# An FFN on one core: the down projection as seven block products, chained partial sums, and norm operands from unscaled sums

## The chip, the cores and the metric

The kernel runs on one core of a Trainium2 chip. The metric is device time in microseconds for one execution; before the change it is 2420.82 us, the median of three runs (2419.04 to 2423.86).

## The reference

Two layers of an encoder are applied to 256 + 512 = 768 token rows (two sequences, same weights), width 1024, in float32:

```python
h = rms_norm(x, g_mix[l]); proj = h @ w_in[l]
# attention on q, k, v of proj; a gated convolution branch on u; gates from gl
x = x + (ga * a + gc * c) @ w_out[l]
h2 = rms_norm(x, g_ffn[l])
gate, up = jnp.split(h2 @ w_gu[l], 2, axis=-1)
x = x + (jax.nn.silu(gate) * up) @ w_down[l]
```

and a last `rms_norm`. The change is in the last three lines: the FFN has 2816 inner columns, worked on as 22 chunks of 128.

## The kernel before

Everything is kept transposed: feature rows on the 128 partitions, the 768 tokens along the free dimension, in two halves of 384 (`HALVES`). A float32 product is made as three matmul passes (`PASSES`) over operands that are split into a rounded part `hi` and a remainder `lo`: hi x hi, hi x lo, lo x hi. The rounding is a ScalarE copy (`act`, line 211), the remainder a subtraction (`sub_lo`, line 214) on POOL for weights and on VectorE or POOL for activations. Operations of VectorE go through a helper and show as line 133.

Weights arrive as 512 KB `Stage` tiles by DMA on SP's queue. A `Unit` is one such tile split into `hi` and `lo` of 1024 columns. A `Quarter` is 512 columns of `hi` and 512 of `lo`, made from one block of a `Quad` (two stages seen as 2 x 2 blocks) or from a sum of blocks; `Quad.total` makes these sums on VectorE. `Weights.pump` loads stages and splits units ahead of use, as long as at most `N_WH` = 8 buffers are live, one split at a time, `W_STEP` of the program's own clock apart. The order of instructions on each queue is the order in which the Python program emits them; `Clock.at` and `Clock.later` place work some microseconds of that clock later, and `tick`, after each `yield` of a body, emits what is due and then calls `pump`.

The gate/up product of a chunk is done as a 2 x 2 x 2 block product with seven block products instead of eight (`seven`, `gu_body`): 7 x 4 x 3 = 84 matmuls of 384 columns. Product 2 is added in the bank of product 1 and product 3 in that of product 5; other sums are made on VectorE when the products come out of PSUM. Chunks 0 and 1 are done together at the start, interleaved; the others one by one. `finish` multiplies silu(gate) by up and splits the result into `acthi` and `actlo`.

The down projection (`down_body`) takes two chunks at a time: 8 output tiles x 2 token ranges (256 and 512 columns) x 2 chunks x 3 passes = 96 matmuls, each result added into the residual `xs` by VectorE. It follows the next gate/up chunk. The last block of a layer takes four chunks (18 to 21), and each `xs` tile that it completes goes into the next norm.

`ffn_norm` makes the operands of the seven products: first half (products 1 and 2) when the first half's scale is known, second half afterwards: operands 4, sums 5, then differences 6, 7 and 3. `Norm.finish` makes the scale: a matmul for the variance, a power on POOL, a transpose on TensorE (`n2var`, `n2R` in the rows), then the scalings on VectorE.

## Time and profile before

| | |
|---|---|
| median of three runs | 2420.82 us |
| the profiled execution | 2421.99 us, span 2420.2 us |
| mean granted TensorE clock | 0.973 |
| TensorE matmul busy | 2274.7 us (94%) |
| VectorE busy | 1669.6 us (69%) |
| POOL busy | 1203.7 us (50%) |
| ScalarE busy | 1008.5 us (42%) |

The span runs from the first to the last instruction. PE is TensorE, PEld its weight loads, DVE VectorE, ACT ScalarE, POOL GpSimd. The FFN lies at about 677 to 1210 us (layer 0) and 1875 to 2409 us (layer 1). Matmuls are pipelined, so that the busy time of one (0.34 us for 384 columns) overlaps that of the next.

### The profile page before, as it was taken

What the parts mean: (1) busy time and instruction counts of PE and PEld (TensorE: products, weight loads), DVE (VectorE), ACT (ScalarE), POOL (GpSimd) and SP (SyncE); (2) the same over time, 40 slices, a digit from 0 to 9 for tenths busy, and PEclk for the clock granted to TensorE, in tenths of its full rate; (3) what the DMA queues carried; (4) which work ended last, traced back from release to release, by engine and by line L of the source; (5) the groups of instructions that cost most, each with busy time, mean ns of one, the idle gap of its engine ahead of it and who ended that gap; (6) DMA issues with size and microseconds to landing.
All of it is one profiled execution on the core that took longest, in us unless ns stands there. A gap on an engine that the chain in (4) does not pass through costs nothing.

```text
span 2420.2 us, 34516 instructions
## 1 busy us (share of the span) xinstructions
PE 2274.7 (94%) x13516; PEld 2101.4 (87%) x13516; DVE 1669.6 (69%) x2272; ACT 1008.5 (42%) x1985; POOL 1203.7 (50%) x864
## 2 busy tenths in 40 slices
...
DMA packets 58019, 177.14 MB, mean 73 GB/s; under 512 B 6528, under 2 KB 13696, under 8 KB 57856
## 3 DMA queue, kind: packets, MB, share of 16 engines
...
q14 instruction: 57, 0.47, 0.1%
...
## 4 chain that ended last, share of the span: by engine, by line
PE 57%; DVE 31%; ACT 4%; POOL 4%; issue 3%; DMA 1%; POOLq 0%; SPq 0%; DVEq 0%; ACTq 0%
DVE L_y L133 22%; PE L_d L203 15%; PE L_c L203 5%; PE L_o L203 4%; PE L_gl L203 4%; PE L_f150m L473 1%; PE L_f70m L473 1%; PE L_f90m L473 1%; PE L_f130m L473 1%; PE L_f50m L473 1%; PE L_f190m L473 1%; PE L_f110m L473 1%; PE L_f170m L473 1%; PE L_f200m L473 1%; PE L_f210m L473 1%
## 5 line engine op out<-in xcount | busy, mean ns | idle before, releaser
L133 DVE SCALAR_TENSOR_TENSOR L_y<-L_z,vec,L_y 128x783 f32<-128x783 f32 x480 | 624.0, 1334 | 2.5
L214 POOL TENSOR_TENSOR wq_L_wgu_0m<-T_L_wgu,wq_L_wgu_0m 128x512 fp32r<-128x512 f32 x168 | 235.4, 1421 | 395.0 <-ACT wq_L_wgu_0m L211 222.2
L211 ACT ACTIVATE wq_L_wgu_0m<-T_L_wgu 128x512 fp32r<-128x512 f32 x168 | 99.7, 625 | 484.8 <-DVE T_L_wgu L133 478.2
L203 PE MATMUL L_d<-L_acthi,lo_L_wd 128*128 128x256 f32 (+1 forms) x704 | 237.8, 338 | 4.5 <-POOL lo_L_wd L214 4.5
L133 DVE TENSOR_TENSOR L_x<-L_d,L_x 128x256 f32<-128x256 f32 (+1 forms) x344 | 183.7, 556 | 82.3 <-PE L_d L203 80.5
L203 PE MATMUL L_d<-L_acthi,hi_L_wd 128*128 128x256 f32 (+1 forms) x704 | 237.1, 337 | 0.0
L203 PE MATMUL L_d<-L_actlo,hi_L_wd 128*128 128x256 f32 (+1 forms) x704 | 236.9, 337 | 0.0
L214 POOL TENSOR_TENSOR wq_L_wgu_0m<-st_L_wgu,wq_L_wgu_0m 128x512 fp32r<-128x512 f32 x126 | 167.3, 1346 | 43.4 <-ACT wq_L_wgu_0m L211 39.6
L203 PE MATMUL L_gl<-L_h1h,hi_L_wgl 128*128 128x512 f32 (+1 forms) x512 | 178.6, 349 | 0.6 <-DVE L_h1t4m L133 0.6
L214 POOL TENSOR_TENSOR lo_L_wgl<-st_L_wgl,hi_L_wgl 128x1024 fp32r<-128x1024 f32 x32 | 104.6, 3276 | 147.8 <-ACT hi_L_wgl L211 147.8
L203 PE MATMUL L_gl<-L_h1h,lo_L_wgl 128*128 128x512 f32 (+1 forms) x512 | 174.9, 342 | 0.0
L203 PE MATMUL L_gl<-L_h1l,hi_L_wgl 128*128 128x512 f32 (+1 forms) x512 | 174.6, 341 | 0.0
L203 PEld LDWEIGHTS L_d<-L_acthi,lo_L_wd 128*128 128x128 f32 x704 | 132.3, 188 | 20.3 <-POOL lo_L_wd L214 5.1
L203 PEld LDWEIGHTS L_d<-L_actlo,hi_L_wd 128*128 128x128 f32 x704 | 132.3, 188 | 14.8
L203 PEld LDWEIGHTS L_d<-L_acthi,hi_L_wd 128*128 128x128 f32 x704 | 132.4, 188 | 14.4
L214 POOL TENSOR_TENSOR lo_L_wqkv<-st_L_wqkv,hi_L_wqkv 128x1024 fp32r<-128x1024 f32 x24 | 67.4, 2815 | 125.7 <-ACT hi_L_wqkv L211 109.3
L133 DVE TENSOR_TENSOR L_silu<-L_silu,L_fu 128x384 f32<-128x384 f32 x88 | 88.7, 1010 | 44.7 <-ACT L_silu L211 43.2
L214 POOL TENSOR_TENSOR lo_L_wd<-st_L_wd,hi_L_wd 128x1024 fp32r<-128x1024 f32 x44 | 105.0, 2405 | 11.6 <-ACT hi_L_wd L211 9.0
L203 PEld LDWEIGHTS L_gl<-L_h1h,lo_L_wgl 128*128 128x128 f32 x512 | 98.1, 192 | 11.4
L203 PEld LDWEIGHTS L_gl<-L_h1h,hi_L_wgl 128*128 128x128 f32 x512 | 98.3, 192 | 10.4 <-DVE L_h1t4m L133 0.8
L203 PEld LDWEIGHTS L_gl<-L_h1l,hi_L_wgl 128*128 128x128 f32 x512 | 98.5, 192 | 9.7
L214 POOL TENSOR_TENSOR lo_L_wu<-st_L_wu,hi_L_wu 128x1024 fp32r<-128x1024 f32 (+1 forms) x32 | 82.9, 2594 | 47.3 <-ACT hi_L_wu L211 47.3
...
## 6 DMA issues: line engine op xcount, KB each, us to landing
st_L_wgu<-w_gu SPq DMA_DIRECT2D x88, 512.0 KB, 4.2
st_L_wd<-w_down SPq DMA_DIRECT2D x44, 512.0 KB, 4.1
st_L_wu<-w_a SPq DMA_DIRECT2D x32, 512.0 KB, 3.5
st_L_wgl<-w_a SPq DMA_DIRECT2D x32, 512.0 KB, 3.4
st_L_wqkv<-w_qkv SPq DMA_DIRECT2D x24, 512.0 KB, 3.5
st_L_wpw<-w_pw SPq DMA_DIRECT2D x16, 512.0 KB, 3.6
st_L_wo<-w_out SPq DMA_DIRECT2D x16, 512.0 KB, 3.7
...
```

Of the source, the lines that this page charges most:

```text
L133: return f(out, *args, **kw)
L203: nc.tensor.matmul(out, lhsT, rhs, start=start, stop=stop)
L211: nc.scalar.activation(out, in_, func, **kw)
L214: engine.tensor_tensor(lo, x, hi.bitcast(F32), op=ALU.subtract)
L473: nc.tensor.matmul(ps, w[a][:, k * P:(k + 1) * P], h.cols(m, k, b), start=at == m and k == 0 and p == 0, stop=k == KH - 1 and p == 2, skip ...
```

## The change

- Chunks 0 to 19 of the down projection are taken four at a time (`down7`): the contraction (4 chunks) is two halves of two chunks, the output 4 + 4 tiles, the tokens 384 + 384, and the 2 x 2 x 2 block product is made with seven products, in the order 1, 7, 6, 4, 5, 2, 3. Each product has 4 banks, and each bank takes 2 x 3 matmuls of 384 columns.
- Products 6, 5 and 3 are added in product 1's banks and product 4 in product 7's (`CHAIN`); the partial sum is added to the residual after each product. Gate/up uses the same chain, with ScalarE copying the first partial sums out; the pair of chunks 0 and 1 has its own (`CHAIN_TWO`).
- The weights of these down blocks are quarters, with sums. The activations of chunks 0 to 19 are kept unsplit; the operands of the seven products are sums and differences of them (`total`), split into `hi` and `lo` in `prepare`.
- Stages, units and quarters share one pool of 12 buffers; two more stages may be loaded ahead; quarters follow each other after 0.9 instead of 1.45 of the program's clock.
- In the FFN norm the sums of the second half are made from the unscaled residual (`before`) while the output projection runs, and are multiplied by the scale afterwards; products are asked for in the order 1, 2, 5, 6, 7, 3, 4.
- The last block of a layer takes two chunks (20 and 21) in the old way.

```diff
--- before.py
+++ after.py
-                self.tile = wpool.tile([P, 1024], F32, name="st_" + self.name, tag="ws", bufs=N_WS)
+                self.tile = wpool.tile([P, 1024], F32, name="st_" + self.name, tag="w", bufs=N_W)
...
-                if self.loaded < len(self.stages) and self.staged < N_WS:
+                ahead = self.live <= N_WH - 2 and self.ready < len(self.all) and self.all[self.ready].size == 1
+                if self.loaded < len(self.stages) and self.staged < N_WS + 2 * ahead:
...
-                assert self.live + w.size <= N_WH
+                assert self.live + w.size + max(self.staged, N_WS) <= N_W
                 self.live += w.size
...
-                self.staged -= w.last
+                self.staged -= sum(stage.last is w for stage in w.stages)
...
-                self.next = max(self.next, clock.now + W_STEP * w.step / 2)
+                self.next = max(self.next, clock.now + W_STEP[w.size - 1])
...
-        def seven(ws, order, h, ready, name, done):
+        def seven(ws, order, chain, h, ready, name, done):
...
-                at = {2: 1, 3: 5}.get(m, m)
+                at = chain.get(m, m)
...
+                if p in self.own:
+                    self.own[p][0](j)
...
-                for j, f in enumerate([scale(j) for j in range(KC + 1)] + self.more[p]):
-                    steps.append(((N_STEPS[3][0] + each[0] * j, N_STEPS[3][1] + each[1] * j), f))
+                after = lambda j: each[0] * j if p not in self.own else N_OWN[0] * j + N_OWN[1] * max(0, j - KH)
+                if p in self.own:
+                    scales = [lambda f=f: f(rstd[0][:, :n]) for f in self.own[p][1]]
+                    more = [lambda f=f: f(rstd[0][:, :n]) for f in self.more[p]]
+                else:
+                    scales, more = [scale(j) for j in range(KC + 1)], self.more[p]
+                for j, f in enumerate(scales + more):
+                    steps.append(((N_STEPS[3][0] + after(j), N_STEPS[3][1] + each[1] * j), f))
...
+                def before(j):
+
+                    k = j % KH
+                    if j < KH:
+                        if k % 2 == 0:
+                            tot[k] = tot[k + 1] = Z(nm(f"hs{k}"))
+                        act(part(k), y.xs[j][:, second], AF.Copy, scale=gain(j))
+                    else:
+                        vector.scalar_tensor_tensor(part(k), y.xs[j][:, second], gain(j), part(k),
+                                                    op0=ALU.mult, op1=ALU.add)
+
+                def low(m, k, t, engine):
+                    norm.low()
+                    norm.lows.append(cut(m, k, t, engine))
+
+                def total(k):
+                    def f(r):
+                        vector.tensor_tensor(part(k), part(k), r, op=ALU.mult)
+                        low(5, k, part(k), vector if k % 2 else nc.gpsimd)
+                    return f
+
                 def more(m, k):
-                    def f():
-                        a11, a12, a21, s = to(k, 0), to(k + KH, 0), to(k, 1), part(k)
-                        d, x, z = {6: (s, s, a11), 7: (a21, a11, a21), 3: (a12, a12, s)}[m]
-                        vector.tensor_tensor(d, x, z, op=ALU.subtract)
-                        norm.low()
-                        norm.lows.append(cut(m, k, d, vector if k % 2 else nc.gpsimd))
+                    def f(r):
+                        a11, a12, s = to(k, 0), to(k + KH, 0), part(k)
+                        if m == 4:
+                            t = to(k + KH, 1)
+                            vector.scalar_tensor_tensor(t, y.xs[k + KH][:, second], gain(k + KH), r,
+                                                        op0=ALU.mult, op1=ALU.mult)
+                        elif m == 7:
+                            t = to(k, 1)
+                            vector.scalar_tensor_tensor(t, y.xs[k][:, second], gain(k), r, op0=ALU.mult, op1=ALU.mult)
+                            vector.tensor_tensor(t, a11, t, op=ALU.subtract)
+                        else:
+                            t, x, z = {6: (s, s, a11), 3: (a12, a12, s)}[m]
+                            vector.tensor_tensor(t, x, z, op=ALU.subtract)
+                        low(m, k, t, vector if k % 2 else nc.gpsimd)
                     return f
 
-                norm = Norm(nm("n2"), y.xs, lambda j: vcol(l, V_GFFN, j), HALVES, out, to=to,
-                            order=[range(KC), [*range(KH, KC), *range(KH)]],
-                            more=[[], [more(m, k) for m in (6, 7, 3) for k in range(KH)]], each=((0.7, 0.0), (0.55, 0.0)))
+                norm = Norm(nm("n2"), y.xs, gain, HALVES, out, to=to,
+                            more=[[], [more(m, k) for m in (6, 7, 3, 4) for k in range(KH)]], each=((0.7, 0.0), (0.55, 0.0)),
+                            own={1: (before, [total(k) for k in range(KH)])})
                 return norm
 
...
+                def done_one(m, e, ps):
                     c = cs[e]
-                    bank = lambda i: banks[e, i][:, :HN]
-                    first, second = slice(0, HN), slice(HN, T)
                     if m == 1:
-                        z = Z(nm(f"fz{c}"))
-                        tmp[e] = z[:, :HN], z[:, HN:T]
-                        act(tmp[e][0], bank(1))
+                        y.silu[c] = U(nm(f"silu{c}"))
+                        act(y.silu[c][:, first], ps)
+                        return
+                    g = y.silu[c]
+                    if m == 7:
+                        y.up[c] = Z(nm(f"fu{c}"))[:, :HN]
+                        act(y.up[c], ps)
+                    elif m == 6:
+                        act(g[:, second], ps)
+                    elif m == 4:
+                        add(g[:, second], ps)
+                        clock.at(0.8, lambda: silu(c, second))
+                    elif m == 5:
+                        add(y.up[c], ps)
+                        clock.at(0.2, lambda: times(c, second, y.up.pop(c)))
                     elif m == 2:
-                        if c not in y.silu:
-                            y.silu[c] = U(nm(f"silu{c}"))
-                        act(y.silu[c][:, first], bank(1), AF.Silu)
+                        add(g[:, first], ps)
+                        clock.at(0.8, lambda: silu(c, first))
+                    else:
+                        times(c, first, ps)
+                        finish(c)
+
...
+                def finish(c):
+                    g = y.acts[c] = y.silu.pop(c)
+                    if c in y.after:
+                        y.after.pop(c)()
+                    if c >= PLAIN:
+                        hi, lo = y.acts[c] = U(nm(f"acthi{c}"), F32R), U(nm(f"actlo{c}"), F32R)
+
+                        def parts():
+                            act(hi, g)
+                            clock.at(1.0, lambda: sub_lo(vector, lo, g, hi))
+                        clock.at(1.5, parts)
 
...
+            def down_cut(stages, r, c):
+                return stages[r - 1].tile[:, (c - 1) * 512:c * 512]
+
+            def down7(order, c0):
+
+
+                pairs = ((c0, c0 + 1), (c0 + 2, c0 + 3))
+                ops, banks, jobs, src = {}, {}, {}, {}
+                half = lambda t, i: t[:, i * HN:(i + 1) * HN]
+                ms = [m for m, e in order if e == 0]
+
+                def operand(m, e):
+
+                    a, b = (y.acts.get(c) for c in pairs[e])
+                    if m in (1, 2, 4):
+                        return {1: lambda: half(a, 0), 2: lambda: half(b, 0), 4: lambda: half(b, 1)}[m]()
+                    s = half(y.dsum, e)
+                    d, x, z, op = {7: lambda: (s, half(a, 0), half(a, 1), ALU.subtract),
+                                   6: lambda: (s, half(b, 1), s, ALU.subtract),
+                                   5: lambda: (half(a, 0), half(a, 0), s, ALU.add),
+                                   3: lambda: (s, half(b, 0), s, ALU.subtract)}[m]()
+                    vector.tensor_tensor(d, x, z, op=op)
+                    return d
+
+                def total(m):
+                    if m == 7:
+                        y.dsum = U(nm(f"dS{c0}"))
+                    src[m] = [operand(m, e) for e in range(2)]
+
+                def prepare(m):
+                    ops[m] = U(nm(f"dh{c0}_{m}"), F32R), U(nm(f"dl{c0}_{m}"), F32R)
+                    jobs[m] = []
+                    for e, x in enumerate(src[m]):
+                        hi, lo = (half(t, e) for t in ops[m])
+                        act(hi, x)
+                        jobs[m].append(clock.later(0.5 + 0.4 * e, lambda x=x, hi=hi, lo=lo: sub_lo(vector, lo, x, hi)))
+
+                def first():
+                    total(1)
+                    total(7)
+                    prepare(1)
+                    clock.at(1.0, lambda: prepare(7))
+
+                def done(m, j, bank):
+                    x = {1: (j, 0), 2: (j, 0), 7: (j + KH, 1), 5: (j + KH, 1), 6: (j, 1), 4: (j, 1), 3: (j + KH, 0)}[m]
+                    x = half(y.xs[x[0]], x[1])
+                    vector.tensor_tensor(x, bank, x, op=ALU.add)
+
+                def body(ws):
+                    for n, m in enumerate(ms):
+                        w = [ws[2 * n], ws[2 * n + 1]]
+                        for f in jobs[m]:
+                            f()
+                        at = CHAIN.get(m, m)
+                        for j in range(KH):
+                            if at == m:
+                                banks[m, j] = PS(nm(f"d{c0}m{m}_{j}"))
+                            ps = banks[at, j][:, :HN]
+                            for e in range(2):
+                                for p, (a, b) in enumerate(PASSES):
+                                    nc.tensor.matmul(ps, w[e][a][:, j * P:(j + 1) * P], half(ops[m][b], e),
+                                                     start=at == m and e == 0 and p == 0, stop=e == 1 and p == 2,
+                                                     skip_group_check=at != m)
+                                    clock.now += HN / 2400.0
+                            if j == KH - 1:
+                                ws.free(2 * n, 2 * n + 1)
+                            done(m, j, ps)
+                            if j == 0 and 0 < n < len(ms) - 1:
+                                prepare(ms[n + 1])
+                            if j == 1 and n < len(ms) - 2:
+                                total(ms[n + 2])
+                            yield
+                    for c in range(c0, c0 + 4):
+                        y.acts.pop(c)
+                tail = c0 == PLAIN - 4
+                y.after[PLAIN if tail else c0 + 2] = lambda: clock.at(
+                    D_AHEAD[tail], first)
                 return body
 
             def down_body(*cs):
...
                         order = [(es, j, p) for p in range(len(parts))
-                                 for es in ((chunks,) if p and l == L - 1 else (chunks[:2], chunks[2:])) for j in range(KC)]
...
             def add_gu(*cs):
-                order = [(m, e) for m in (1, 4, 5, 6, 7, 2, 3) for e in range(1)]
-                if len(cs) > 1:
-                    order = [(m, e) for m in (1, 2, 4, 5, 6, 7, 3) for e in range(len(cs))]
+                ms, chain = (ORDER, CHAIN) if len(cs) == 1 else (ORDER_TWO, CHAIN_TWO)
+                order = [(m, e) for m in ms for e in range(len(cs))]
                 units = weights.add_quads(nm(f"wgu{cs[0]}"), [[w_gu[l, b + c] for b in (0, NFF)] for c in cs],
                                           gu_cut, order)
-                stream.put([(l, f"gu:{c}") for c in cs], units, gu_body(order, *cs))
+                stream.put([(l, f"gu:{c}") for c in cs], units, gu_body(order, chain, *cs))
+
+            def add_down7(c0):
+                order = [(m, e) for m in ORDER for e in range(2)]
+                units = weights.add_quads(nm(f"wd{c0}"), [[w_down[l, c0 + 2 * e + i] for i in range(2)] for e in range(2)],
+                                          down_cut, order)
+                stream.put([(l, f"down:{c0}")], units, down7(order, c0))
 
             def add_down(*cs):
                 stream.add([(l, f"down:{c}") for c in cs], nm(f"wd{cs[0]}"), [w_down[l, c + e] for c in cs for e in range(2)],
                            down_body(*cs))
 
             add_gu(0, 1)
-            for c in range(2, NFF, 2):
+            for c in range(2, NFF):
                 add_gu(c)
-                if c < NFF - 2:
-                    add_down(c - 2)
-                add_gu(c + 1)
-            add_down(NFF - 4, NFF - 2)
+                if c % 4 == 3 and c < PLAIN - 1:
+                    add_down7(c - 3)
+            add_down7(PLAIN - 4)
+            add_down(PLAIN)
             return y
 
         def sigmoids(y):
...
+D_AHEAD = (4.0, 8.0)
+
+ORDER, CHAIN = (1, 7, 6, 4, 5, 2, 3), {6: 1, 5: 1, 3: 1, 4: 7}
+ORDER_TWO, CHAIN_TWO = (1, 2, 5, 6, 7, 3, 4), {6: 1, 7: 1, 4: 1, 3: 5}
...
+PLAIN = 20
...
-W_STEP = 2.9
+W_STEP = (0.9, 2.9)
...
+N_OWN = (0.5, 0.45)
...
+N_W = 12
```

## Rows read from the trace of the kernel before

**Rows 1.** The page, part 1: busy time and its share of the span

```profile
PE 2274.7 (94%) x13516; PEld 2101.4 (87%) x13516; DVE 1669.6 (69%) x2272; ACT 1008.5 (42%) x1985; POOL 1203.7 (50%) x864
```

**Rows 2.** The chain of waits, FFN of layer 0: start us, us, what

```profile
838.72 16.74 PE L_d L203 x96
870.23 14.62 PE L_f80m L473 x84
```

**Rows 3.** Busy time by stage, FFN of layer 0 (stage, length, engines, clock, DMA)

```profile
839.00:1162.00 323.00, 323.00 (x1848) 306.82 (x1847) 179.05 (x283) 96.97 (x169) 166.29 (x114) 1.00 0.20 66
```

**Rows 4.** Waits of TensorE, 650 to 730 us: total, times, longest

```profile
PE L_f00m L473 <- POOL L_h L214: 3.0, 3, 2.0
...
PE L_f00m L473 <- ACT wq_L_wgu_0m L211: 2.0, 1, 2.0
PE L_f01m L473 <- ACT wq_L_wgu_1m L211: 1.2, 1, 1.2
PE L_f01m L473 <- POOL wq_L_wgu_1m L214: 1.1, 2, 0.8
...
PE L_f00m L473 <- POOL wq_L_wgu_0m L214: 0.8, 1, 0.8
```

**Rows 5.** Busy time by stage, the FFN's start after the second scale

```profile
688.00:729.00 41.00, 32.94 (x141) 29.39 (x141) 35.08 (x48) 18.35 (x35) 29.48 (x23) 0.81 0.11 39
```

**Rows 6.** Timeline of TensorE at the seam: start, us, line, what, idle before

```profile
1221.99 0.66 PE L207 MATMUL L_n1R<-ident,L_n1rb 128*128 128x128 f32 x4 [2.60 <-DVE L_n1rb L133]
```

**Rows 7.** Timeline of TensorE at the end of the kernel

```profile
2410.24 0.89 PE L203 MATMUL nfvar<-ones,nfss 128*128 128x2 f32 x4 [1.84 <-DVE nfss L133]
```

**Rows 8.** VectorE's groups by shape, whole run: busy us, mean ns, idle before

```profile
L133 DVE TENSOR_TENSOR L_x<-L_d,L_x 128x512 f32<-128x512 f32 x176 | 120.6, 687 | 79.1 <-PE L_d L203 78.3
L133 DVE TENSOR_TENSOR L_silu<-L_silu,L_fu 128x384 f32<-128x384 f32 x88 | 88.7, 1010 | 44.7 <-ACT L_silu L211 43.2
L133 DVE TENSOR_TENSOR L_x<-L_d,L_x 128x256 f32<-128x256 f32 x168 | 69.8, 418 | 3.2 <-PE L_d L203 2.2
...
L133 DVE TENSOR_TENSOR T_L_wgu<-st_L_wgu,T_L_wgu 128x512 f32<-128x512 f32 x88 | 60.9, 692 | 8.8 <-DVE T_L_wgu L133 0.5
...
L133 DVE TENSOR_TENSOR L_x<-L_o,L_x 128x384 f32<-128x384 f32 x32 | 17.8, 555 | 80.6 <-PE L_o L203 80.6
...
L133 DVE TENSOR_TENSOR L_hs<-L_hr 128x384 f32<-128x384 f32 x8 | 6.5, 810 | 0.3
L133 DVE SCALAR_TENSOR_TENSOR L_x<-L_x,vec,nfR 128x512 f32<-128x512 f32 x8 | 5.9, 742 | 0.5 <-PE nfR L207 0.5
...
L133 DVE SCALAR_TENSOR_TENSOR L_n1t<-L_x,vec,L_n1R 128x256 f32<-128x256 f32 x8 | 3.6, 474 | 0.5 <-PE L_n1R L207 0.5
```

**Rows 9.** Timeline of POOL in the FFN, three subtractions in a row

```profile
867.43 4.15 POOL L214 TENSOR_TENSOR wq_L_wgu_0m<-T_L_wgu,wq_L_wgu_0m 128x512 fp32r<-128x512 f32 x3 [4.79 <-ACT wq_L_wgu_0m L211]
```

**Rows 10.** ScalarE's groups by shape, whole run

```profile
L211 ACT ACTIVATE wq_L_wgu_0m<-st_L_wgu 128x512 fp32r<-128x512 f32 x126 | 72.2, 621 | 0.0
...
L211 ACT ACTIVATE L_h<-L_hr 128x384 fp32r<-128x384 f32 x40 | 20.2, 520 | 15.8 <-DVE L_hr L133 15.6
```

**Rows 11.** The page, part 6: DMA issues, KB each, us to landing

```profile
st_L_wd<-w_down SPq DMA_DIRECT2D x44, 512.0 KB, 4.1
```

**Rows 12.** Timeline of VectorE, beside idle POOL and in that stretch

```profile
839.35 0.56 DVE L133 TENSOR_TENSOR L_silu<-L_silu,L_fu 128x384 f32<-128x384 f32 x1
...
868.98 1.43 DVE L133 TENSOR_TENSOR L_silu<-L_silu,L_fu 128x384 f32<-128x384 f32 x1 [0.77 <-ACT L_silu L211]
870.34 0.55 DVE L133 TENSOR_TENSOR L_fu<-L_f70m,L_fz 128x384 f32<-128x384 f32 x1
```

**Rows 13.** Timeline of TensorE, seven matmuls of a gate/up chunk

```profile
868.68 1.38 PE L473 MATMUL L_f70m<-L_h,wq_L_wgu_0m 128*128 128x384 f32 x7
```

**Rows 14.** Waits of TensorE, whole run

```profile
PE L_d L203 <- POOL lo_L_wd L214: 4.5, 3, 1.8
```

116 lines of the change are left out of this document (59 added, 57 removed).

## The prediction

> **What bounds the kernel now.** I read the page's busy line first [rows 1]: TensorE is busy for 94% of the span, so in most stages TensorE's own issue rate is the time. I then read the chain of waits through the FFN [rows 2]: gate/up chunk follows gate/up chunk and down pair follows down pair with no gap, each entry on TensorE. A chunk of 84 matmuls of 384 columns takes 14.63 us, or 0.174 us a matmul; a down pair of 96 matmuls (256 and 512 columns in turn, 384 on average) takes 16.74 us, the same rate. The stage table [rows 3] says how much cover is there: over 323 us of FFN TensorE is never idle at full granted clock, VectorE is busy for 55%, POOL for 51%, ScalarE for 30%. So removed matmuls come back as time there at full price, as long as VectorE and POOL keep up. Three places are not like that: the start of the FFN, where TensorE idles and the granted clock averages 0.81 [rows 4, 5], the seam between the layers [rows 6], and the end [rows 7].
>
> **What is removed.** Four chunks of the down projection are 2 x 96 = 192 matmuls, 2 x 16.74 = 33.5 us. After it they are 7 products x 4 banks x 2 halves of the contraction x 3 passes = 168 matmuls of 384 columns, 168 x 0.174 = 29.2 us. That is 4.2 us a group; five groups a layer (chunks 0 to 19) and two layers make 10 groups: 42 us. Chunks 20 and 21 stay as they are. Gate/up keeps its 84 matmuls a chunk.
>
> **What is added beside TensorE.** Weights of a group: before, 4 ScalarE roundings and 4 POOL subtractions of 1024 columns; after, 14 of 512 each, and 8 weight differences on VectorE at 0.69 us [rows 8]. POOL then has 7 x 4 + 14 = 42 subtractions of 1.30 us [rows 9] = 55 us in 88 us of matmuls (4 x 14.7 + 29.2). ScalarE's 14 roundings of the weights (0.62 us) and 14 of the operands (0.52 us) [rows 10], 16 us, fit easily beside the 30% it has. Loads are the same 512 KB transfers; a group's four are asked for earlier or later by a few products, and 4.1 us to land [rows 11] is under the two products (8.4 us) by which weights are made ahead: nothing, and if that cover went, some 4 us a group.
>
> VectorE in a group's 29.2 us: 28 evictions of 384 columns at 0.555 us = 15.5 us (the row for a sum out of PSUM of that shape [rows 8]); 6 operand sums and 10 operand remainders, all with both inputs in SBUF; some 4 weight differences of the next chunk. If the two-input ones run freely (0.56 us [rows 12]) this is 15.5 + 9.0 + 2.8 = 27.3 us: just fits. But the same product takes 1.43 us when it starts inside a POOL subtraction [rows 9, 12], and 1.01 us on average over the run [rows 8]. VectorE's queue is in order, so this matters where TensorE waits for its result.
>
> That place is the second half of products 6 and 5 in the order 1, 7, 6, 4, 5, 2, 3. There the program puts on VectorE: the eviction of bank 1, two sums for the product after next, then the two remainders of the next operand. TensorE's product lasts 24 x 0.174 = 4.18 us. Its second bank ends at 2.09 us, plus 0.17 us since a matmul lasts 0.34 while the next starts after 0.174 [rows 13]; with the eviction VectorE is free for the sums at 2.82 us. Three two-input operations later the first remainder is there, one more later the second. TensorE needs the first at its second matmul of the next product (4.35 us), the second 3 matmuls later. So the stall is 4w - 2.05 us, w being the mean time of such an operation: 0.2 us at w = 0.56, 2.0 at 1.01, 3.7 at 1.43. In a product of 4.2 + 1.5 us POOL has two subtractions, 2.6 us or 46% of it, so w = 0.56 + 0.46 x 0.87 = 0.96 and the stall 1.8; if only one of the four meets POOL (the first subtraction is over when the sums start), w = 0.78 and the stall 1.1. I take 1.5 us, twice a group: 3.0 us, 30 us in all; the ends are 4 us and 73 us. Behind the waiting remainders stand the evictions of banks 2 and 3, whose banks TensorE next writes two products later (over 4 us): no second stall. The other products have no sums ahead of the remainders: 2.82 + 2 x 0.96 = 4.7 against 4.9, nothing.
>
> Which operations are slowed can be read in one place: the 1.43 us product started inside one of three POOL subtractions in a row, while the sum after it, with one input in PSUM, took 0.55 us beside the same POOL work [rows 9, 12]. The Trainium skill (SBUF — State Buffer, section Who interferes with whom) says that a VectorE instruction with two SBUF inputs contends with a GpSimd instruction that reads SBUF and that the second to issue blocks fully until the first ends; by that rule the trace agrees, and the rule speaks against this change, which adds two-input work and POOL work at once.
>
> **Gate/up with chained banks.** A product now writes a bank that ScalarE or VectorE has just read. Between the two uses stands another product, 12 x 0.174 = 2.09 us, against a read of 0.5 to 0.56 us: nothing while both queues are in order, and VectorE has less there than before (per chunk 5 operations of 384 instead of 7, and the 768-wide remainder is gone). ScalarE's reads now stand behind roundings that wait for weight differences (at most 2 x 0.69 + 0.62 us, still under 2.09). If this cover were lost, each 0.5 us late would cost 0.5 us x 40 chunks = 20 us.
>
> **The FFN norm.** From the second half's scale on, the stage is VectorE's: 35.1 us busy in 41 us [rows 5]. TensorE waits there 3.0 us for POOL's remainders of the first operand and 2.0 + 1.2 + 1.1 + 0.8 us for weights, 8.1 us in all, and stretches at the lower clock (1.2 of 2.4 GHz) cost another (1 - 0.81) x 41 = 7.8 us [rows 4, 5]. The change takes four sums of 0.81 us from this stage (3.2), adds four products out of PSUM (2.2) and three remainders on VectorE (at a sum's 0.81, 2.4), and takes four sums out of PSUM from the first two chunks (2.2) [rows 8]: VectorE has about 1 us less, and the 3.0 us on the first operand go, since both engines share its remainders. The four added products ahead of the scale lie in the output projection, where VectorE waits 80.6 us for TensorE in the run [rows 8]: free. I take -4 us a layer, -8 in all; ends +3 a layer (one more half-clock stretch) and -16 a layer (all of both).
>
> **First down block, seam, end.** TensorE waits 4.5 us in three places for the remainder of a down weight [rows 14]; smaller pieces made earlier: -3 (0 to -4.5). At the seam the last block has two chunks instead of four, so its second part lasts 11 us instead of 22, while VectorE has 8 sums and 5 added squares of the same shape (0.69), 8 scalings and 4 remainders (0.47) [rows 8] = 14.6 us: it comes 3.5 us late, and TensorE, already idle there for 2.60 us [rows 6], waits that much longer (0 to +8). At the end the last part shrinks from 11.2 to 5.6 us, but VectorE's 8 x 0.42 + 5 x 0.42 + 8 x 0.74 = 11.4 us [rows 8] don't: about 3 us of the removed time don't come (+3, 0 to +5).
>
> **The sum.** The profiled execution took 2421.99 us (span 2420.2, the rest is outside it). 2422.0 - 42 + 30 - 8 - 3 + 3.5 + 3 = 2405.5. The median of the runs is 1.2 us below the profiled one: 2404 us.
>
> **Rivals.** First, the cover holds: VectorE's two-input operations meet POOL rarely in the two tight products. For it: POOL's second subtraction may fall behind the sums, and the down weights' own differences are all made before the block. Then the stall is 0.4 us a group: 2422 - 42 + 4 - 8 - 3 + 6.5 = 2379, 2365 to 2392.
>
> Second, slower: VectorE and POOL block each other in these products every time. For it: if such operations and POOL's subtractions exclude each other, they need 14 x 1.30 + 16 x 0.56 + 4 x 0.69 = 29.9 us of the block's 29.2, and 55 + 26 x 0.56 + 24 x 0.69 = 86 of the group's 88. Against it: weights can be made ahead in the gate/up chunks. It decides from 42 + 8 + 3 - 6.5 = 46.5 us, 4.65 a group, 2.3 a tight product, so from w = 1.09, not far over the run's mean of 1.01; at 1.43 the time is 2448, and around 2437 when most of them block.
>
> Third, no change: w near 1.05 uses up the gain: 2416 to 2426. That the matmuls would not go is no rival: their count follows from the loops.
>
> **How the numbers follow.** Forecast (2390 to 2416) 0.45, cover holds 0.25, no change 0.11, slower 0.19. A run tells 0.2%, 4.8 us, from no change, so faster means under 2416. A little of the forecast's case reaches into the band: faster 0.68, same 0.13, slower 0.19. The range takes most of the first rival and half of the slower one: 2370 to 2432.
>
> **What would show it.** Right: down blocks of 30 to 33 us with TensorE waiting for VectorE's operand remainders at the start of products 4 and 2, VectorE over 85% busy in them, gate/up chunks still at 14.7 us, the FFN's start some 4 us shorter. The first rival shows as 29.3 us blocks without a wait; the second as blocks over 34 us, or a granted clock under 1.0 inside the FFN. Wrong would be waits for banks or weights instead, or gate/up chunks that grow.

## The result: 1.7% slower

The changed kernel takes 2462.13 us (median of four runs, 2461.06 to 2466.5) against 2420.3 us for the kernel before on the same chip: ratio 1.0174, interval 1.0156 to 1.0191. The forecast was 2404 us, with a range up to 2432: the change is slower where it was expected to be faster.

The page, part 1 of the changed kernel (busy time, share of the span, instructions), answers to [rows 1]. TensorE has 240 matmuls fewer and is busy 12 us less, and yet the span is 39.6 us longer: 2459.8 against 2420.2.

```profile
PE 2263.0 (92%) x13276; PEld 2122.5 (86%) x13276; DVE 1805.7 (73%) x2426; ACT 1139.0 (46%) x2281; POOL 1302.9 (53%) x958
```

Split by stage, cut at the first and last matmuls, the 39.6 us are:

| stage, both layers together | before | after | difference |
|---|---|---|---|
| FFN norm: gate/up of chunks 0 and 1 | 101.4 | 113.5 | +12.1 |
| chunks 2 to 21 and the whole down projection | 965.9 | 988.7 | +22.8 |
| seam to the first FFN matmul of layer 1 | 663.8 | 665.9 | +2.1 |
| after the last down matmul | 11.8 | 14.5 | +2.7 |

The chain of waits through the same FFN answers to [rows 2] (start, us, what). Gate/up chunks are as before, 14.63 us without a gap. A down block is no longer one entry on TensorE: its start is a chain through VectorE's and ScalarE's queues.

```profile
764.58 0.63 ACT wq_L_wd_0m L211
766.22 0.95 DVE T_L_wd L133
767.25 0.69 DVE T_L_wd L133
767.95 0.77 DVE L_x L133 x2
768.79 1.74 DVE L_dS L133 x2
770.87 1.01 DVE L_x L133 x2
773.93 2.76 DVE L_dl L133 x2
776.73 23.01 PE L_d0m L1171 x116
799.74 14.62 PE L_f40m L481 x84
```

The stage table answers to [rows 3] and [rows 5] (stage, length, engines, granted clock): one down block, the stretch in it after the stall, and the FFN norm stage. The block lasts 36.5 us where its 168 matmuls need 29.2. The granted clock in it averages 0.91, because after the stall it is at the lower of its two levels (1.2 GHz; 0.56 in a window cut slightly wide). The ten blocks last 35.5 to 39.6 us, 367.7 us together, 75 us over their matmuls.

```profile
763.20:799.74 36.54, 33.38 (x170) 32.01 (x170) 31.83 (x54) 13.17 (x26) 18.25 (x13) 0.91 0.18 58
776.00:782.50 6.50, 6.26 (x22) 5.77 (x21) 4.97 (x10) 0.93 (x2) 4.33 (x4) 0.56 0.00 0
677.60:734.10 56.50, 41.00 (x178) 37.88 (x177) 48.18 (x60) 23.53 (x46) 36.24 (x30) 0.82 0.12 38
```

TensorE's timeline at the stall, between products 7 and 6 (the third of the block). Seven matmuls of [rows 13] take 1.38 us; here six take 3.9. The first waits for ScalarE's rounded operand, the next ones for VectorE's remainders, and from there on matmuls follow each other in 0.32 us instead of 0.174 until 781.4.

```profile
773.66 0.44 PE L1171 MATMUL L_d0m<-L_dh,wq_L_wd_0m 128*128 128x384 f32 x1 [1.86 <-ACT L_dh L211]
775.16 0.69 PE L1171 MATMUL L_d0m<-L_dl,wq_L_wd_0m 128*128 128x384 f32 x1 [1.06 <-DVE L_dl L133]
...
776.73 0.69 PE L1171 MATMUL L_d0m<-L_dl,wq_L_wd_1m 128*128 128x384 f32 x1 [0.24 <-DVE L_dl L133]
777.21 0.52 PE L1171 MATMUL L_d0m<-L_dh,wq_L_wd_1m 128*128 128x384 f32 x1
```

What the other engines do meanwhile. VectorE's timeline, with the weight differences T, the operand sums L_dS and the operand remainders L_dl:

```profile
762.37 1.32 DVE L133 TENSOR_TENSOR T_L_wd<-st_L_wd 128x512 f32<-128x512 f32 x1
...
768.79 2.15 DVE L133 TENSOR_TENSOR L_dS<-L_silu,L_dS 128x384 f32<-128x384 f32 x2
...
771.80 0.68 DVE L133 TENSOR_TENSOR T_L_wd<-st_L_wd,T_L_wd 128x512 f32<-128x512 f32 x1
...
773.93 2.75 DVE L133 TENSOR_TENSOR L_dl<-L_dS,L_dh 128x384 fp32r<-128x384 f32 x2
```

ScalarE's timeline, the rounding of a weight quarter and that of product 6's operand behind it:

```profile
772.57 0.63 ACT L211 ACTIVATE wq_L_wd_0m<-T_L_wd 128x512 fp32r<-128x512 f32 x1 [3.89 <-DVE T_L_wd L133]
773.10 0.92 ACT L211 ACTIVATE L_dh<-L_dS 128x384 fp32r<-128x384 f32 x2
```

GpSimd's (POOL's) timeline, subtractions of down weights:

```profile
768.75 1.31 POOL L214 TENSOR_TENSOR wq_L_wd_1m<-T_L_wd,wq_L_wd_1m 128x512 fp32r<-128x512 f32 x1 [2.15 <-ACT wq_L_wd_1m L211]
773.27 1.42 POOL L214 TENSOR_TENSOR wq_L_wd_0m<-T_L_wd,wq_L_wd_0m 128x512 fp32r<-128x512 f32 x1 [3.21 <-ACT wq_L_wd_0m L211]
774.64 1.62 POOL L214 TENSOR_TENSOR wq_L_wd_1m<-T_L_wd,wq_L_wd_1m 128x512 fp32r<-128x512 f32 x1
```

Six of the eight weight differences T of the block stand on VectorE between 762 and 773.5 us, in among the first evictions and the sums L_dS. Product 4's difference (771.80) is late; its rounding on ScalarE waits 3.89 us for it, and the rounding of product 6's operand stands behind that in ScalarE's queue although its sums were done at 770.9. When ScalarE gets going, the weight quarters come in a row, GpSimd subtracts them in a row, and the two remainders that TensorE is waiting for start beside these subtractions. One by one they are:

```profile
773.93 1.18 DVE L133 TENSOR_TENSOR L_dl<-L_dS,L_dh 128x384 fp32r<-128x384 f32 x1
775.03 1.64 DVE L133 TENSOR_TENSOR L_dl<-L_dS,L_dh 128x384 fp32r<-128x384 f32 x1
```

The first ends (775.11) 0.4 us after one GpSimd subtraction has ended (774.69), the second (776.67) 0.4 us after the next (776.26). In all ten blocks they take 1.18 and 1.64 us, to 0.01 us.

### The profile page after: what moved, and what is told of

It is laid out like the page before. It is cut to its first block, busy times and chain, and to the rows that moved or that the text cites. A ratio compares the mean times of both kernels' runs of the same rounds, so it can differ in the third digit from the quotient of the medians.

```text
span 2459.8 us, 34620 instructions
## 1 busy us (share of the span) xinstructions
PE 2263.0 (92%) x13276; PEld 2122.5 (86%) x13276; DVE 1805.7 (73%) x2426; ACT 1139.0 (46%) x2281; POOL 1302.9 (53%) x958
## 4 chain that ended last, share of the span: by engine, by line
PE 48%; DVE 40%; ACT 5%; issue 3%; POOL 2%; DMA 1%; DVEq 0%; POOLq 0%; SPq 0%; ACTq 0%
DVE L_y L133 24%; PE L_c L203 5%; PE L_o L203 4%; PE L_gl L203 3%; DVE T_L_wd L133 2%; PE L_d8m L1171 2%; PE L_d0m L1171 2%; PE L_d16m L1171 2%; PE L_d4m L1171 2%; DVE L_dl L133 2%; PE L_d12m L1171 2%; DVE L_x L133 2%; PE L_f190m L481 1%; PE L_f130m L481 1%; PE L_f200m L481 1%
## 5 line engine op out<-in xcount | busy, mean ns | idle before, releaser
L214 POOL TENSOR_TENSOR wq_L_wgu_0m<-st_L_wgu,wq_L_wgu_0m 128x512 fp32r<-128x512 f32 x126 | 177.0, 1409 | 67.8 <-ACT wq_L_wgu_0m L211 67.8
L214 POOL TENSOR_TENSOR lo_L_wu<-st_L_wu,hi_L_wu 128x1024 fp32r<-128x1024 f32 (+1 forms) x32 | 82.9, 2595 | 52.3 <-ACT hi_L_wu L211 50.7
L214 POOL TENSOR_TENSOR lo_L_wo<-st_L_wo,hi_L_wo 128x1024 fp32r<-128x1024 f32 x16 | 39.5, 2469 | 125.6 <-ACT hi_L_wo L211 125.6
L211 ACT ACTIVATE wq_L_wgu_0m<-st_L_wgu 128x512 fp32r<-128x512 f32 x126 | 79.2, 629 | 57.2 <-issue 25.8
L214 POOL TENSOR_TENSOR wq_L_wd_0m<-T_L_wd,wq_L_wd_0m 128x512 fp32r<-128x512 f32 x40 | 57.7, 1442 | 81.9 <-ACT wq_L_wd_0m L211 81.9
L203 PE MATMUL L_o<-L_mThi,hi_L_wo 128*128 128x384 f32 x256 | 88.0, 344 | 6.6 <-ACT L_mThi L211 6.6
L214 POOL TENSOR_TENSOR lo_L_wpw<-st_L_wpw,hi_L_wpw 128x1024 fp32r<-128x1024 f32 x16 | 40.1, 2505 | 100.2 <-ACT hi_L_wpw L211 95.5
L203 PE MATMUL L_ug<-L_h1h,lo_L_wu 128*128 128x256 f32 (+1 forms) x256 | 87.9, 343 | 2.7 <-DVE lo_L_wu L133 2.7
L203 PE MATMUL L_c<-L_zsh,hi_L_wpw 128*128 128x256 f32 (+1 forms) x256 | 90.3, 353 | 0.0
L203 PE MATMUL L_ug<-L_h1h,hi_L_wu 128*128 128x256 f32 (+1 forms) x256 | 89.0, 348 | 0.0
L203 PE MATMUL L_ua<-L_h1h,hi_L_wu 128*128 128x256 f32 (+1 forms) x256 | 88.9, 347 | 0.0
```

Of the source, the lines that this page charges most:

```text
L203: nc.tensor.matmul(out, lhsT, rhs, start=start, stop=stop)
L211: nc.scalar.activation(out, in_, func, **kw)
L214: engine.tensor_tensor(lo, x, hi.bitcast(F32), op=ALU.subtract)
```

## The experiments

Lengths of blocks and chunks are from the first to the last matmul. "Chunk" is the gate/up chunk ahead of a block (the first of layer 0); the last block of each layer follows chunk 21 and stands apart. A norm stage goes from the first matmul of chunk 0 to the first of chunk 2. Each ratio is to runs of the kernel before on the same chip.

| run | us | ratio (95% interval) | blocks | last blocks | chunk | norm stages |
|---|---|---|---|---|---|---|
| before | 2420 | 1 | pairs, 16.9 | | 15.3 | 51.4, 50.0 |
| the change | 2462 | 1.017 (1.016, 1.019) | 35.5-37.0 | 39.6, 38.8 | 14.8 | 56.6, 56.8 |
| normonly | 2426 | 1.001 (1.000, 1.002) | pairs | | 15.2 | 53.6, 53.1 |
| pairs | 2490 | 1.028 (1.026, 1.030) | pairs | | 19.0 | 56.6, 56.8 |
| nodiff | 2404 | 0.992 (0.990, 0.994) | 30.8-30.9 | 31.9, 31.2 | 14.8 | 56.7, 55.4 |
| warm | 2455 | 1.014 (1.012, 1.016) | 35.3-35.4 | 40.2, 38.8 | 14.8 | 56.6, 57.0 |
| step | 2672 | 1.103 (1.101, 1.105) | 48.4-50.4 | 53.5, 52.1 | 16.8 | 54.9, 52.3 |
| hold | 2486 | 1.027 (1.025, 1.029) | 36.7-39.2 | 41.7, 42.0 | 14.8 | 58.6, 56.6 |
| tahead | 2435 | 1.005 (1.004, 1.007) | 31.3-31.4 | 36.9, 35.6 | 16.7 | 56.6, 56.8 |
| diffpool | 2494 | 1.030 (1.029, 1.032) | 39.3-39.4 | 42.1, 41.3 | 14.8 | 58.7, 56.6 |
| oldnorm | 2465 | 1.016 (1.014, 1.018) | 35.7-37.0 | 40.5, 41.3 | 14.8 | 55.1, 54.9 |
| t1 | 2464 | 1.016 (1.014, 1.017) | 35.1-36.7 | 39.3, 40.5 | 14.9 | 56.6, 57.0 |
| nolo | 2402 | 0.990 (0.989, 0.992) | 29.8-30.1 | 34.9, 33.9 | 14.8 | 56.6, 56.8 |
| t4 | 2440 | 1.008 (1.006, 1.009) | 30.8-31.4 | 32.2, 31.1 | 18.4 | 56.6, 55.6 |
| pairstep | 2439 | 1.007 (1.006, 1.009) | 30.8-31.4 | 32.3, 31.1 | 17.9 | 55.0, 52.3 |
| best | 2442 | 1.009 (1.007, 1.010) | 30.8-31.8 | 31.9, 31.1 | 20.6 | 53.7, 53.2 |
| besttail | 2448 | 1.010 (1.008, 1.012) | 30.8-31.6 | 33.2, 32.4 | 20.3 | 53.1, 53.2 |

### Halves of the change: pairs and normonly

The run pairs takes the seven products away and leaves the rest of the change:

```diff
-                if c % 4 == 3 and c < PLAIN - 1:
-                    add_down7(c - 3)
-            add_down7(PLAIN - 4)
-            add_down(PLAIN)
+                if c < NFF - 2:
+                    add_down(c - 2)
+                add_gu(c + 1)
+            add_down(NFF - 4, NFF - 2)
...
-PLAIN = 20
+PLAIN = 0
```

> The changed kernel with the down projection put back to pairs of chunks and a last block of four; the new FFN norm, the chained gate/up, the shared weight pool and the 0.9 step stay. Theory: of the 42 us lost, the down blocks with their half-clock stretches make up some 25 to 30, seam and end 7, the FFN's start (56.5 us instead of 51.4 in layer 0) 10 in both layers. So this kernel loses only the last part: 2430 us, 10 above before, with down pairs of 16.7 us and no fall of the clock between 740 and 1180 us. Rival: the chained banks or the shared pool cost something in the steady stretch, which then shows here as gate/up chunks over 14.7 us or pairs over 16.8 us and 2440 us or more.

It took 2489.5 us: the rival. The chunk after each pair grew, to 19.0 us in nine of eighteen places and to 17.5 in the others. Product 6 now writes a bank that ScalarE must have copied out, and TensorE waits 1.9 us for that copy; in the nine longer chunks the granted clock then falls to its lower level for a time (TensorE's timeline in the first: 36 matmuls in 8.10 us):

```profile
777.51 8.10 PE L481 MATMUL L_f30m<-L_h,wq_L_wgu_0m 128*128 128x384 f32 x36 [1.94 <-ACT L_silu L211]
```

ScalarE itself is idle before it. The copy (776.99) stands in its queue behind a weight rounding that waits 3.8 us for GpSimd, which has five subtractions of weight quarters in a row there (ScalarE's timeline):

```profile
776.45 0.63 ACT L211 ACTIVATE wq_L_wgu_0m<-st_L_wgu 128x512 fp32r<-128x512 f32 x1 [3.76 <-POOL wq_L_wgu_0m L214]
776.99 0.47 ACT L211 ACTIVATE L_silu<-L_f30m 128x384 f32<-128x384 f32 x1
```

So the chained banks cost nothing only while no rounding ahead of the copy waits that long. In the changed kernel none does (all chunks 14.75 to 14.79 us); undone by half, the change is worse than whole. As a control for the down blocks this run is not clean.

The run normonly is the kernel before with the new norm and the new order of chunks 0 and 1.

```diff
+                            own={1: (before, [total(k) for k in range(KH)])})
...
-                    order = [(m, e) for m in (1, 2, 4, 5, 6, 7, 3) for e in range(len(cs))]
+                    order = [(m, e) for m in ORDER_TWO for e in range(len(cs))]
...
+N_OWN = (0.5, 0.45)
+ORDER_TWO, CHAIN_TWO = (1, 2, 5, 6, 7, 3, 4), {6: 1, 7: 1, 4: 1, 3: 5}
```

> The kernel before with the new FFN norm alone (operands from unscaled sums, order 1, 2, 5, 6, 7, 3, 4 and its chain for the pair of chunks 0 and 1); weight quarters still follow each other after 1.45 of the program's clock. Theory N1: the norm's own order is what lengthens the FFN's start, since it puts three more remainders a layer on VectorE: start 56 us, total 2430 us. Theory N2: the norm is sound, and the start is longer because quarters split after 0.9 put weight work ahead of the operands on VectorE and POOL: here the start is 45 to 51 us and the total 2410 to 2420 us.

The norm stages grew by 2.3 and 3.1 us, where the forecast took 4 off each; the whole, 2426 us, lies between the two theories.

### Cause or symptom: nodiff and warm

nodiff leaves the weight differences out: product quarters that need one take a plain quarter instead.

```diff
             def total(self, i):
+                if "wd" in self.name:
+                    return self.cut(self.stages, 1 + i % 2, 1 + i // 3)
```

> The changed kernel without the differences of down weights: the 8 VectorE subtractions of 512 columns a group are left out and a plain block of the weights is used in their place, so the down projection's result is another one; all other work is the same. Theory: the stall before product 6 comes from VectorE's backlog at the start of the block, most of which are these subtractions, and it reaches TensorE through ScalarE, whose rounding of the operand stands behind a rounding that waits for such a difference. Then the blocks take 29.5 to 31 us without a fall of the clock, and the total is about 2405 us. Rival: the chain of operand sums and remainders against POOL is enough for the stall; blocks still 34 us or more, total over 2440 us.

Blocks of 30.8 us at full clock, 2404 us. The differences are what the stall hangs on. The remainders of product 6's operand are slow here too (2.30 us for both), but in the eight blocks ahead of the last ones they come early enough for product 6. What is left there is one wait of 0.62 to 0.67 us, at the start of product 4 (waits of TensorE in the first block, and VectorE's timeline: the remainders for product 6, then two sums and the remainders for product 4):

```profile
PE L_d0m L1173 <- DVE L_dl L133: 0.6, 1, 0.6
```

```profile
769.71 2.30 DVE L133 TENSOR_TENSOR L_dl<-L_dS,L_dh 128x384 fp32r<-128x384 f32 x2
...
774.26 1.88 DVE L133 TENSOR_TENSOR L_silu<-L_silu,L_dS 128x384 f32<-128x384 f32 x2
776.06 1.01 DVE L133 TENSOR_TENSOR L_dl<-L_silu,L_dh 128x384 fp32r<-128x384 f32 x2
```

warm adds 18 matmuls with zeros at the end of product 7, that is, into the stall:

```diff
+                            if n == 1 and j == KH - 1:
+                                for _ in range(WARM):
+                                    nc.tensor.matmul(ps, zero, half(ops[m][0], 0), start=False, stop=True,
+                                                     skip_group_check=True)
...
+WARM = 18
```

> The changed kernel with 18 matmuls of 384 columns by a tile of zeros added at the end of product 7 of each down block (in the bank it has just summed, which they leave as it is), 3.1 us, about as long as TensorE idles there. Theory: the fall of the granted clock in the block follows from this idle time, and costs 3.4 us after it; with the idle time filled the clock stays at 2.4 GHz there, the blocks take 33 us instead of 36.4 and the total is about 2430 us. Rival: the clock falls for another reason or the wait only moves behind the added matmuls: blocks of 36 us or more, 2460 us or more.

The block with 186 matmuls is 1.2 us shorter than that with 168, and its granted clock stays at 1.00 (stage table):

```profile
762.66:798.00 35.34, 33.53 (x188) 32.51 (x188) 32.04 (x54) 13.30 (x26) 18.25 (x13) 1.00 0.17 60
```

So the fall of the clock hangs on the idle time and is no second cause. It is worth more than the 1.2 us: 18 x 0.174 = 3.1 us of matmuls were added, more than the 2.2 us from the last matmul before the stall to the first behind it. The theory's 33 us and 2430 us were missed all the same. 186 x 0.174 = 32.4 us, so the block is 2.9 us over its matmuls, and 1.7 of these are waits for VectorE's remainders: 0.8 us at product 6 and 0.9 at product 4. The changed kernel's block has no wait at product 4; this part moved behind the added matmuls, as the rival said. The last blocks, which stall longer, did not gain.

### Where in the queues: step, hold, tahead, diffpool, t1

> The changed kernel with the old spacing of the weight quarters, 1.45 us of planned time between two of them in place of 0.9; nothing else. Theory: of the 12 us by which the two FFN norm stages grew, some 5.4 are the new order of the norm (run normonly), and the rest is GpSimd, which with the closer spacing turns to weight quarters between the remainders that the first two chunks wait for. Expected: norm stages of 53.5 us each in place of 56.7, the down blocks as they are (35 to 39 us), 2456 us. Rival: the rest is the chained gate/up pair beside the down blocks' weights, which come later anyway: norm stages of 56.5, and wider spacing makes the weights of the down blocks late: blocks of 38 us and 2470 or more.

```diff
-W_STEP = (0.9, 2.9)
+W_STEP = (1.45, 2.9)
```

The norm stages did as expected (54.9 and 52.3). The blocks starved, far beyond the rival's 38 us and 2470 us: TensorE waits in the first block for the weights of three products, 0.6 to 1.6 us at a time. The planner looks once per bank, 0.96 us of planned time; at 0.9 it may split a quarter per bank, at 1.45 only one in two banks, 14 in a block of 28 banks, and that is just what the block uses up. So the closer spacing is a part of the change that the block cannot do without.

> The changed kernel with one edit: the end of a block's first product holds back the next weight quarter by 0.8 us of planned time, so that ScalarE gets the two operand roundings of product 6 ahead of a weight rounding that waits for a difference on VectorE. No work is left out, and VectorE has as many instructions as before. Theory (order of ScalarE's queue): the wait on the rounded operand, 2.2 us a block and 4.9 in the last, goes; what is left is the remainders' wait of 1.5 us; the fall of the granted clock becomes shorter; blocks of 33 to 34 us in place of 36.7, 2435 us. Rival (VectorE is simply behind, and the queue's order is its shadow): the wait moves to the remainders of product 6 or to the weights of product 4, blocks of 35.5 to 37, 2455 to 2465 us.

```diff
+                            if n == 0 and j == KH - 1:
+                                weights.next = max(weights.next, clock.now + HOLD)
...
+HOLD = 0.8
```

The wait for the rounded operand went, as the theory said, but the time did not: the block's waits are now all on VectorE's remainders. ScalarE's order was only how VectorE's lateness showed. The rival held, and the time was worse still than it said. Alone this run does not decide it, since a difference is made in the same step as its rounding and so was held back with it; t1 below shows the same shift with differences that are earlier (waits of TensorE in one block, total, times, longest, first of the changed kernel):

```profile
PE L_d0m L1171 <- ACT L_dh L211: 1.9, 1, 1.9
PE L_d0m L1171 <- DVE L_dl L133: 1.3, 2, 1.1
```

and of hold:

```profile
PE L_d0m L1171 <- DVE L_dl L133: 5.4, 4, 1.9
```

> The changed kernel with the differences of the down weights put on VectorE up to two quarters earlier, as soon as their tiles are there; as many instructions, none left out. Theory (a rounding that waits for its difference holds ScalarE's queue): the difference is done when the rounding comes, so ScalarE doesn't wait; blocks of 33 to 34 us, 2435 us. Rival (VectorE is behind): earlier differences delay VectorE's reads of the first banks and the sums just as much, blocks of 35.5 to 37, 2455 to 2465 us. If the tiles aren't there earlier, nothing changes at all.

```diff
                 w.make(engines)
+                for u in self.all[self.ready + 1:self.ready + 1 + T_AHEAD]:
+                    if u.size == 1 and "wd" in u.quad.name and self.here(u):
+                        u.quad.operand(u.m)
...
+T_AHEAD = 2
```

With nothing left out and only the place of the differences changed, the blocks fell to 31.3 us, 27 us off the whole. What is left of the stall is one wait of 0.8 us, except in the last blocks, which still wait 2.5 us for a remainder. But the chunk ahead of the block grew from 14.8 to 16.7, at a granted clock of 1.00: four differences now stand ahead of VectorE's read of product 5 in that chunk, and product 3 may not write the bank before it (waits of TensorE in tahead, one chunk and the block after it):

```profile
PE L_f30m L484 <- DVE L_fu L133: 1.6, 1, 1.6
PE L_d0m L1174 <- DVE L_dl L133: 0.8, 1, 0.8
```

That the theory's 2435 us came out is luck: the blocks are 2 us shorter than it said, and ten chunks 1.6 to 1.9 us longer.

> As the run tahead, but the differences of the down weights are put on VectorE at most one quarter early in place of two. Theory: tahead's blocks of 31.3 us came from differences that are ready when ScalarE turns to them, and its chunks 3, 7, 11 and 15 grew because those differences stand ahead of VectorE's read of product 5's bank (a wait of 1.6 us each, then a lower granted clock). One quarter early is 2 us later: the chunks lose less and the blocks stay under 32.5: 2425 to 2432 us. Rival: one quarter is too late for the rounding again, blocks of 33 to 35 us, 2440 to 2455 us.

```diff
-T_AHEAD = 2
+T_AHEAD = 1
```

One quarter early is too late: blocks as in the changed kernel, longer even than the rival's 33 to 35 us. The rival's reason is not the one, though. The wait for the rounded operand is gone, and TensorE waits as long for VectorE's remainders instead (waits of TensorE in the first block):

```profile
PE L_d0m L1174 <- DVE L_dl L133: 3.3, 2, 3.0
```

The chunks lost next to nothing (14.9 to 15.4 us); four of the differences stand in the block again.

> The changed kernel with the eight differences a block of the down weights on GpSimd in place of VectorE. Theory (VectorE is behind by the six differences that fall into the block's start): GpSimd has room, 18 of 36 us busy in a block, so the result is near that of the kernel without these differences: blocks of 31.5 to 33 us, 2415 us. Rival (what slows VectorE is GpSimd's work beside it, 0.56 against 1.43 us for a two-input pass in the trace of before): more GpSimd work slows the subtractions that are left, and the weights come late behind 1.4 us differences: blocks of 35 to 38, 2450 to 2475 us.

```diff
-                    vector.tensor_tensor(t, x, z, op=ALU.subtract)
+                    (nc.gpsimd if "wd" in self.name else vector).tensor_tensor(t, x, z, op=ALU.subtract)
```

39.4 us a block, past even the rival's 35 to 38. A difference takes GpSimd 1.3 to 1.6 us, and each stands in its queue between two remainders of quarters; the rounding that waits for it holds product 6's operand 4.4 us long. GpSimd has idle time in the block, but not in this chain.

### What makes VectorE late: nolo

In this run GpSimd's subtraction for the down weights is a fill with zeros; the remainders of those weights are left out of the products.

```diff
-                sub_lo(engines[0], lo, src, hi)
+                if "wd" in self.name:
+                    nc.gpsimd.memset(lo.bitcast(F32), 0.0)
+                else:
+                    sub_lo(engines[0], lo, src, hi)
```

> The changed kernel with GpSimd's subtraction that makes the remainders of the down weights of the seven-product blocks replaced by a fill with zeros: this work is left out (the product of that remainder adds nothing). The differences stay on VectorE, as late as in the changed kernel. Rival theory (GpSimd beside VectorE is what makes VectorE late: differences take 1 to 1.8 us in place of 0.68, subtractions 1.4 in place of 0.5): blocks fall to 31 to 32 us, 2410 us. Theory (the differences' place in VectorE's queue is the cause, their length secondary): the six differences still stand ahead of the sums; some of the wait goes, blocks of 33 to 35, 2435 to 2450 us.

The rival held in eight of the ten blocks: 29.8 us (30.1 in one), their matmuls and half a microsecond, with all differences on VectorE in the same places. The last block of each layer still waits 1.8 us for the rounded operand and lasts 34.9 and 33.9 us. VectorE's timeline, to be read beside the lines of the changed kernel above; here the two remainders end after 1.01 us together:

```profile
762.89 0.68 DVE L133 TENSOR_TENSOR T_L_wd<-st_L_wd 128x512 f32<-128x512 f32 x1
...
768.35 1.01 DVE L133 TENSOR_TENSOR L_dS<-L_silu,L_dS 128x384 f32<-128x384 f32 x2
...
770.21 0.68 DVE L133 TENSOR_TENSOR T_L_wd<-st_L_wd,T_L_wd 128x512 f32<-128x512 f32 x1
...
772.35 1.01 DVE L133 TENSOR_TENSOR L_dl<-L_dS,L_dh 128x384 fp32r<-128x384 f32 x2
```

The remainders' group over the whole run (busy us, mean ns), in the changed kernel:

```profile
L133 DVE TENSOR_TENSOR L_dl<-L_dS,L_dh 128x384 fp32r<-128x384 f32 x60 | 50.7, 884 | 0.5 <-ACT L_dh L211 0.5
```

and in nolo:

```profile
L133 DVE TENSOR_TENSOR L_dl<-L_dS,L_dh 128x384 fp32r<-128x384 f32 x60 | 32.1, 576 | 0.5 <-ACT L_dh L211 0.5
```

Counted from the block's first matmul, the late difference comes 2.7 us earlier (at 5.9 instead of 8.6 us), the two remainders take 1.01 us instead of 2.75, and the stall is gone from these eight blocks. The fill is also shorter than the subtraction (0.53 us against 1.3) and waits for no rounding. That is not all of it: two fills (772.52 and 773.05) run beside the two remainders of 772.35 and leave them at their free length. The rule of the Trainium skill that the prediction weighed (SBUF — State Buffer, section Who interferes with whom: whichever of a two-input VectorE instruction and a GpSimd instruction that reads SBUF comes second waits until the first is over) fits both: a fill reads nothing, and the two remainders of the changed kernel each end 0.4 us after a GpSimd subtraction inside which they started.

### Can the differences be early and free: t4, pairstep, best, besttail

> As the run tahead, but the differences of the down weights are put on VectorE up to four quarters early in place of two. Theory: with two quarters the blocks are at 31.3 us and chunks 3, 7, 11 and 15 lose 2.2 us each because four differences stand ahead of VectorE's read of product 5's bank; with four, six of the eight differences are made while VectorE still has idle stretches in the chunk (2 us in a row in the trace of tahead), so the chunks are back near 14.8 us and the blocks stay: 2434 less 8 times 2, 2418 us. Rival: the differences then wait for their tiles to land and hold VectorE's queue, chunks of 17 us or more and 2435 to 2450 us.

```diff
-T_AHEAD = 2
+T_AHEAD = 4
```

The blocks stay at 31, the last blocks come down to 32.2 and 31.1, and the chunks ahead of the blocks grow to 17.2 to 19.1 us: the rival's size. VectorE's idle stretches are used up, and the operand's remainders again meet GpSimd, now in the chunk (VectorE's timeline in t4: 1.6 us a remainder; it is busy for 13.9 of 14.6 us there).

```profile
849.43 3.24 DVE L133 TENSOR_TENSOR L_dl<-L_silu,L_dh 128x384 fp32r<-128x384 f32 x2
...
855.99 0.55 DVE L133 TENSOR_TENSOR L_fu<-L_f70m,L_fu 128x384 f32<-128x384 f32 x1
```

> As the run t4, with the spacing of weight quarters at 1.45 us of planned time for the first two gate/up chunks alone and 0.9 for all others. Theory: GpSimd's quarters between the remainders of the norm are the close spacing's doing: norm stages of 54.9 and 52.3 us as in the run step, without that run's late weights in the down blocks: 6 us under t4. Rival: with 1.45 the first chunks' quarters only come later and the third chunk waits: the same as t4 within 2 us.

```diff
+W_PAIR = 1.45
...
-                self.next = max(self.next, clock.now + W_STEP[w.size - 1])
+                self.next = max(self.next, clock.now + (W_PAIR if w.size == 1 and "wgu0" in w.quad.name else W_STEP[w.size - 1]))
```

> As the run pairstep, with the FFN norm and the first two gate/up chunks as before the change. If the norm's new order costs 2.3 and 3.1 us a layer (run normonly) and adds to the spacing, the norm stages are back at 51.4 and 50.0 us: 5.5 us under pairstep, some 2406 us, 0.6% under the kernel before. Rival: the old order's stage needs the old place of all later quarters as well and stays at 54 to 55 us: as pairstep, or slower.

```diff
-                             own={1: (before, [total(k) for k in range(KH)])})
+                             order=[range(KC), [*range(KH, KC), *range(KH)]],
...
-ORDER_TWO, CHAIN_TWO = (1, 2, 5, 6, 7, 3, 4), {6: 1, 7: 1, 4: 1, 3: 5}
+ORDER_TWO, CHAIN_TWO = (1, 2, 4, 5, 6, 7, 3), {2: 1, 3: 5}
```

pairstep's norm stages are 55.0 and 52.3, as expected, but the next chunk grew by 3.5 us in each layer (2439 against 2440 us in all). In best, with the old norm as well, the stages are 53.7 and 53.2. In both, TensorE waits there for weight quarters (in best 5.7 us for ScalarE's in chunk 1) instead of operand remainders: both rivals held. Neither setting moved more than 3 us of the whole. What comes late changes with the order; what the stage wins, the chunks behind it lose.

> As the run best, with the operands of the last block of each layer started 4 us of planned time after chunk 20 in place of 8, as in the other blocks. Theory: the last block is 3 to 5 us longer than the others because its first sums and roundings fall, with chunk 21's, into its start; 4 us earlier they fall into chunk 21, where VectorE has idle stretches: last blocks of 32 to 33 us in place of 36 and 35, 6 us under best. Rival: they collide in chunk 21 with the passes that split chunk 20's activations, and chunk 21 grows by as much: the same within 2 us, or slower.

```diff
-D_AHEAD = (4.0, 8.0)
+D_AHEAD = (4.0, 4.0)
```

The last blocks are 1.3 us longer than in best, where earlier differences had already put them right (31.9 and 31.1 us, not the 36 and 35 that the theory starts from), and chunk 21 grew by 1.2 us: the rival.

> The changed kernel with the FFN norm and the first two gate/up chunks as before the change: scaled second half, then sums, and the old order and banks of the two chunks. The down blocks, the other chunks and the spacing of 0.9 stay. Runs so far give 5.4 us for the new norm alone (both layers, at the old spacing) and 6.3 us for the spacing alone (with the new norm). Theory (two costs that add up, both on GpSimd): the norm stages fall from 56.7 to 53.9 us each, 2456 us. Rival (one cost, the close spacing only hurts the new norm, whose remainders stand in GpSimd's queue later): the stages are back at 51.4 and 50.0 us, 2450 us. Second rival: the new norm is what makes the spacing bearable, and the old one is slower at 0.9: stages over 57 us, 2463 us or more.

Its edit is the one shown for best, on the changed kernel. The changed kernel with the old norm keeps stages of 55 us, between theory and second rival: 2465 us, not faster than the change. Of the 12 us that the norm stages grew, 8.6 are there with the old norm and the closer spacing, 5.3 with the new norm and the old spacing; together they are 12.1, so they share 2.

## Why the prediction was wrong

Between the forecast's sum (2405.5 us) and the profiled run (2461.6) lie 56 us. By the stage table 38 of them are in the chunks and the down blocks (+22.8 against -15) and 20 in the norm (+12.1 against -8); seam and end gave 2 back.

**The matmuls.** Right. 0.174 us a matmul holds; nolo's blocks are 29.8 us.

**VectorE's stall.** This is the main step that failed, and it failed twice. First in place and cause: it was forecast at products 4 and 2, from two sums ahead of two remainders. There the changed kernel waits in two of its ten blocks (0.2 and 1.1 us). The stall stands at product 6, from six weight differences that the prediction had put ahead of the block: "the down weights' own differences are all made before the block", "the two products (8.4 us) by which weights are made ahead". The trace shows them inside it, and the quarter of product 6 rounded at 768.0 for a product due at 771.6: less than one product ahead. The path that the prediction followed to TensorE never had these six, 6 x 0.69 us, in the block's first 10 us. nodiff, tahead and t1 show that this is the cause. The wait that was forecast does exist, and is small: nodiff shows it once a block, at product 4, with 0.62 to 0.67 us. Two sums and two remainders take 1.88 + 1.01 us there, so w = 0.72, for which 4w - 2.05 gives 0.8. Second in size: w was taken at 0.78 to 0.96 us on the ground that GpSimd is busy 46% of the time. But GpSimd's subtractions come in a row exactly when late differences let ScalarE go on, so the two remainders met it in every block and took 1.18 and 1.64 us, about the slow row of [rows 12]. That this, too, was needed for the stall is shown by nolo. Neither is enough alone, by the eight blocks ahead of the last ones: remainders as slow but differences earlier or left out (tahead, nodiff) leave at most 1.0 us of waits, differences as late but remainders free (nolo) at most 0.3. Loss in ten blocks: 75 us against 30, above the upper end of 73 that the prediction had worked out and then left out of the range.

**The granted clock.** The prediction named a clock under 1.0 as a sign of its second rival, and gave it no price. Of the 7.3 us by which the block shown is over its matmuls, 3.2 are waits; the other 4 are matmuls at less than full rate, most of them at 0.32 us after the stall. By the mean clocks, 0.959 of 2459.8 us against 0.973 of 2420.2, it is 101 us' worth of clock against 65, part of it while TensorE idles. In this block, which was at full clock, 3.2 us of waits cost 7.3.

**Gate/up with chained banks.** Right for the changed kernel: all chunks 14.79 us, and those before the blocks even 0.15 to 0.5 under before. The price for lost cover, 0.5 us a chunk, was too low: in pairs it is 2.7 us a chunk, and 4.2 where the granted clock falls as well (0.91 over such a chunk), in tahead 1.6 to 1.9 us at a clock of 1.00 (not at a lower one, as the expectation of t1 has it).

**The FFN norm.** -8 forecast, +12 measured. The three added remainders are there; what failed is the length of VectorE's operations, and a price that the sum did not have. VectorE is busy for 48.2 us in the stage instead of 39.8 (stage tables above and, for the kernel before, below; 60 operations instead of 56). Its ten remainders of operands take 1.0 and 1.26 us on average where seven took 0.94 and 0.74, and its weight differences take 13.1 us instead of 8.4. That they meet GpSimd more often, with which VectorE now shares the remainders, is likely but was not tested alone. TensorE waits 9.1 us for GpSimd's remainders, instead of the 3.0 of [rows 4] that were to go, and 2.8 us for ScalarE to copy out a bank of the new chain; the waits for weights of [rows 4] are gone. The price that was missing is that of the closer spacing of weight quarters, worth 6 to 9 of the 12 us.

```profile
677.30:728.67 51.37, 39.65 (x179) 35.49 (x178) 39.81 (x56) 20.04 (x39) 34.51 (x29) 0.83 0.12 42
```

Waits of TensorE in that stage of layer 0, changed kernel:

```profile
PE L_f00m L481 <- POOL L_h L214: 9.1, 5, 2.6
PE L_f00m L481 <- ACT L_fu L211: 2.8, 1, 2.8
```

**First block, seam, end.** Right. The waits of [rows 14] are gone; the seam cost 2.1 us (forecast 3.5), the end 2.7 (forecast 3). At the seam the wait moved from the transposes of [rows 6] to the sum ahead of them (waits of TensorE there):

```profile
PE L_n1var L203 <- DVE L_n1ss L133: 4.0, 1, 4.0
PE L_n1R L207 <- DVE L_n1rb L133: 0.3, 1, 0.3
```

**The second rival** is what happened in outcome: blocks over 34 us and a lower clock, with a time past even its 2437 to 2448 us. Its mechanism, VectorE and GpSimd blocking each other, is right, its place is not, and it had 0.19.

**Open.** No kernel that does all the work beat the kernel before; of those with the seven products tahead comes nearest, at 1.005. Whether differences made evenly over the three chunks ahead would give nolo's blocks without longer chunks was not tried. Why the old norm with the old spacing for its chunks does not come back to 51.4 and 50.0 us in best is not settled.
